# Two causal attentions: the multiplication of the exponentials by 1/sum moves from VectorE (DVE) to GpSimd (POOL)

## The chip, the cores and the metric

One Trainium2 chip, one of its cores. The metric is the device time of one execution in microseconds (us), taken as the median of several runs. The engines' names are those of the profile: PE is TensorE (matmuls and transposes), PEld its weight loads, DVE is VectorE, ACT is ScalarE, POOL is GpSimd, SP issues transfers.

## The reference

The program is a stack of four layers on 512 tokens of width 1024, all in float32. Layer 0 projects the tokens, selects keys with an indexer (top-k), attends with 8 heads of 64 and adds a short convolution; layer 1 is a latent attention with 16 heads; layers 2 and 3 are a differential and a neighbourhood attention. Layers 0 and 1 each end in an MLP. The change touches the softmax of layers 0 and 1 only. For each head and each block of 128 query rows the reference computes

```python
logits = jnp.where(causal[None, None], logits, -jnp.inf)
p = jax.nn.softmax(logits, axis=-1).astype(v.dtype)
return jnp.einsum('bhqs,bshd->bqhd', p, v)
```

Here the softmax is exp(scale * logit - max) divided by its sum over the keys; that division, done as a multiplication of the exponentials by a reciprocal, is what the change is about.

## The kernel before

The order of instructions on each engine is written out by hand: the program is emitted in one sequence, each engine executes its own instructions in the order in which they were emitted, and semaphores make an instruction wait for its inputs.

**Weights.** Every weight matrix comes from HBM in units of up to 128x1104 float32. `WeightStream.split` (L262) turns a unit into two halves: ACT rounds it (`w_hi`, L272) and POOL subtracts (`w_lo`, L273). A split is issued by `tick`, which `whole` calls after the matmuls of a piece of other work (L685). Splits run ahead of their use by a ring of four units.

**The attention.** `Net.causal` (L702) handles both attentions. A unit of its work is a head and a block of 128 query rows; block i sees (i+1)*128 keys, so a unit has 128, 256, 384 or 512 columns. Layer 0 has 8 heads x 4 blocks = 32 units (first all heads with blocks 0 and 1, then all with blocks 2 and 3), layer 1 has 16 x 4 = 64. The loop runs in steps; at step t five units are in work:

- A, the newest: PE computes the scores q.k into PSUM (`sp`);
- B, one step later: DVE adds the mask and takes the row maximum (L720, tile `at_nb`), ACT takes the exponential with its row sum (L406, `X<-sp,at_nb`);
- Dn, two steps later: DVE takes the reciprocal of the sum (L728, `at_rs`) and multiplies the exponentials by it in place (L730, `X<-X,at_rs`); the exponentials stand in one of three buffers `P`;
- T, three steps later: PE transposes the normalised block in pieces of 128 columns (L738, `tp`), ACT rounds the result (`pt`, L406), DVE subtracts for the low half (`low`, L409);
- G, four steps later: PE multiplies with v (L760, `mm`).

Within a step the code emits A, then T, then a piece of other matmuls (`fill`: convolution projections in layer 0, the next heads' q, k, v in layer 1) together with its weight split, then B and Dn interleaved: mask, reciprocal, exponential, multiplication. Then `s.due()` issues delayed work, among it what POOL does for the attention: the low halves `ql` of q (layer 1), `cvl` of the convolution (layer 0) and `yl` of the attention's output. Then come `low`, the evacuation of the piece, and G.

Of the kernel before, what the change touches and what calls it, by code (L numbers as in the profile page):

```python
# [16 lines left out]
OP = mybir.AluOpType  # L17
# [356 lines left out]
class Net:  # L374
# [327 lines left out]
    def causal(s, units, qk, scale, mask, vs, pt, out, P, tmp, ofs, wide, fill, extra=lambda t: None):  # L702

        nc = s.nc
        st, of, hold = {}, {}, {}
        N = len(units)

        def A(u):
            h, i = u
            n = max(256, (i + 1) * 128)  # L710
            ps = s.sp.tile([128, 512], F32, name="sp")
            qk(h, i, ps[:, :n], n)
            st[u] = {"s": ps, "n": (i + 1) * 128}

        def B(u, t):
            d = st[u]
            n = d["n"]
            d["P"] = P[t % 3]
            nb, d["sm"] = [s.rope.tile([128, 1], F32, name=f"at_{k}", bufs=4) for k in ("nb", "s")]
            nc.vector.tensor_tensor_reduce(d["s"][:, :n], d["s"][:, :n], mask(u[1]), -scale, 3e38, OP.add, OP.min, nb)  # L720
            yield
            s.act(d["P"][:, :n], d["s"][:, :n], AF.Exp, bias=nb, scale=-1.0, acc=d["sm"])
            yield

        def Dn(u):
            d = st[u]
            rs = s.rope.tile([128, 1], F32, name="at_rs", bufs=4)
            nc.vector.reciprocal(rs, d["sm"])  # L728
            yield
            nc.vector.tensor_scalar(d["P"][:, :d["n"]], d["P"][:, :d["n"]], rs, None, OP.mult)  # L730
            yield

        def T(u):
            h, i = u
            d = st[u]
            tp = s.tp.tile([128, 4, 128], F32, name="tp")
            for k in range(i + 1):
                nc.tensor.transpose(tp[:, k, :], d["P"][:, k * 128:(k + 1) * 128], s.ident)  # L738
            q = (i % 2) * 128
            H, L = [x[:, :i + 1, q:q + 128] for x in pt(h, i // 2)]  # L740
            s.act(H, tp[:, :i + 1, :], AF.Copy)
            d["lo"] = L, tp[:, :i + 1, :], H

        def low(u):
            if u:
                s.sub_lo(*st[u]["lo"])

        def G(u):
            h, i = u
            if i % 2 == 0:  # L750
                return
            c0, c1 = (0, 512) if wide else (i // 2 * 256, i // 2 * 256 + 256)
            if i == 1 or not wide:
                of[h] = s.mm.tile([128, 512], F32, name="mm")
            ps = of[h]
            o = ps[:, (i // 2) * 256:(i // 2) * 256 + 256]
            b = pt(h, i // 2)
            for k in range(i + 1):
                for w in range(2):
                    nc.tensor.matmul(o, vs(h, k), b[w][:, k, :], start=(k == 0 and w == 0), stop=(k == i and w == 1))  # L760
            if i == 3 or not wide:
                hp = (h % 2) * 64
                s.act(tmp[0:64, c0:c1], ps[64:128, c0:c1], AF.Copy)

                def add():
                    nc.vector.tensor_tensor(ofs[hp:hp + 64, c0:c1], ps[0:64, c0:c1], tmp[0:64, c0:c1], OP.add)

                def write():
                    H, L, f = out(h // 2, c0, c1, ofs[:, c0:c1])
                    s.act(H, f, AF.Copy)  # L770
                    s.sub_lo(L, f, H, nc.gpsimd)

                s.defer(add)
                if h % 2 == 1:
                    s.defer(write, 2)

        for t in range(N + 4):
            u = [units[t - k] if 0 <= t - k < N else None for k in range(5)]
            pcs = fill.get(t, [])
            if u[0]:  # L780
                A(u[0])
            if u[3]:
                T(u[3])
            for mm, _ in pcs:
                s.whole(mm)
            bb = B(u[1], t) if u[1] else iter(())
            dn = Dn(u[2]) if u[2] else iter(())
            for x in (bb, dn, bb, dn):
                next(x, None)
            s.due()  # L790
            low(u[3])
            for _, ev in pcs:
                ev()
            if u[4]:
                G(u[4])
                del st[u[4]]
            extra(t)
        s.drain()
# [1527 lines left out]
```

## Time and profile before

| | |
|---|---|
| time, median of 3 runs (range) | 3223.96 us (3220.66 to 3226.64) |
| the profiled execution | 3223.14 us, its span 3221.3 us |
| PE busy | 3067.4 us (95%) |
| DVE, ACT, POOL busy | 2132.6 (66%), 1605.0 (50%), 1473.9 us (46%) |
| attention of layer 0, 187 to 306 us | PE waits 5.6 us for the multiplication |
| attention of layer 1, 800 to 950 us | PE waits 14.4 us for the multiplication |

The two last rows are sums over the waits of PE in those stretches. The busy share of PE counts matmuls whose ends are modelled, so the waits say more about PE than the busy share does. The profiled execution took 1.8 us more than its span, which is the time before its first and after its last instruction, and it lies inside the range of the three runs.

### The profile page before, as it was taken

To read this page: it belongs to the slowest core of one execution; us is meant where nothing else is said; L and a number is where in the kernel's file an instruction comes from. 1 tells how busy PE (TensorE), PEld (TensorE's weight loads), DVE (VectorE), ACT (ScalarE), POOL (GpSimd) and SP (SyncE) were. 2 spreads that over 40 slices of the span, in tenths; PEclk is the share of its full clock that TensorE was granted. 3 is DMA by queue.
4 is the path that set the end of the run, shared out by engine and by line. 5 is a ranking of instruction groups with operands and counts; after the bars stand their busy time and mean duration, and the time that the engine had idled before them with its cause. 6 is when DMAs were issued, how large, how long until landed. Compare 5 with 4: busy or idle time off the path is not lost.

```text
span 3221.3 us, 58548 instructions
## 1 busy us (share of the span) xinstructions
PE 3067.4 (95%) x22868; PEld 2882.8 (89%) x22868; DVE 2132.6 (66%) x4241; ACT 1605.0 (50%) x3795; POOL 1473.9 (46%) x1296
## 2 busy tenths in 40 slices
PE   7999999998889999999999999998999999999989
PEld 7888889887788898789999999998999999999988
DVE  4886444556874344656777877788455777777864
ACT  4544533335665333455555555555325555555552
POOL 4432344443333444465544654462355444444444
PEclk9999999999999999999999999999999999999999
DMA  3122333433123344331221222123323322323334
GB/s 122 60 73 73 106 129 126 150 95 99 37 65 107 125 144 136 111 94 52 63 65 60 62 63 65 60 62 95 116 98 97 84 81 75 88 80 89 88 91 138
DMA packets 96128, 291.93 MB, mean 91 GB/s; under 512 B 19166, under 2 KB 28638, under 8 KB 92780
## 3 DMA queue, kind: packets, MB, share of 16 engines
q1 hardware_dynamic: 89148, 259.01, 24.8%
q0 software_dynamic: 5120, 25.17, 3.6%
q10 hardware_dynamic: 1584, 4.00, 0.4%
q8 instruction: 181, 2.97, 0.4%
q14 instruction: 95, 0.78, 0.1%
HBM read 244.05 MB, written 18.92 MB: 82 GB/s over the span
## 4 chain that ended last, share of the span: by engine, by line
PE 49%; DVE 13%; ACT 4%; issue 4%; DMA 3%; POOL 2%; SPq 0%; POOLq 0%; DVEq 0%; ACTq 0%
PE mm L578 13%; PE mm L580 12%; PE mm L579 12%; PE mm L2101 3%; DMA KL<-KL 1%; POOL w_lo L273 1%; PE tp L2239 1%; ACT X L406 1%; PE tp L2088 1%; DVE s L2051 1%; PE mm L2254 1%; PE mm L2249 1%; DVE X L2232 1%; PE s L2040 1%; DVE ge L1765 1%
## 5 line engine op out<-in xcount | busy, mean ns | idle before, releaser
L273 POOL TENSOR_TENSOR w_lo<-w_raw,w_hi 128x1024 fp32r<-128x1024 f32 (+2 forms) x350 | 879.0, 2517 | 1019.7 <-ACT w_hi L272 994.5
L578 PE MATMUL mm<-w_hi,hh 128*128 128x256 f32 (+3 forms) x2880 | 840.0, 292 | 7.9 <-ACT df_sq L406 2.6
L579 PE MATMUL mm<-w_lo,hh 128*128 128x256 f32 (+3 forms) x2880 | 820.3, 285 | 11.3 <-POOL w_lo L273 11.3
L580 PE MATMUL mm<-w_hi,hl 128*128 128x256 f32 (+3 forms) x2880 | 821.3, 285 | 3.3 <-POOL hl L409 3.0
L578 PEld LDWEIGHTS mm<-w_hi,hh 128*128 128x128 f32 x2880 | 550.5, 191 | 19.3 <-ACT df_sq L406 8.5
L579 PEld LDWEIGHTS mm<-w_lo,hh 128*128 128x128 f32 x2880 | 551.2, 191 | 18.4 <-POOL w_lo L273 13.8
L580 PEld LDWEIGHTS mm<-w_hi,hl 128*128 128x128 f32 x2880 | 549.6, 191 | 6.4 <-POOL hl L409 5.5
L272 ACT CAST w_hi<-w_raw 128x1024 fp32r<-128x1024 f32 (+2 forms) x355 | 366.1, 1035 | 206.0 <-PE mm L580 171.3
L578 PE MATMUL mm<-hh,w_hi 128*128 128x256 f32 (+1 forms) x1408 | 455.3, 323 | 3.0 <-DVE M L1083 2.8
L579 PE MATMUL mm<-hl,w_hi 128*128 128x256 f32 (+1 forms) x1408 | 448.3, 318 | 0.6
L580 PE MATMUL mm<-hh,w_lo 128*128 128x256 f32 (+1 forms) x1408 | 446.8, 317 | 1.2 <-DVE w_lo L273 1.2
L578 PEld LDWEIGHTS mm<-hh,w_hi 128*128 128x128 f32 x1408 | 265.9, 189 | 30.9 <-issue 5.2
L579 PE MATMUL mm<-w_lo,gh 128*128 128x256 f32 x1024 | 287.1, 280 | 1.4 <-POOL w_lo L273 1.4
L578 PE MATMUL mm<-w_hi,gh 128*128 128x256 f32 x1024 | 287.6, 281 | 0.0
L580 PE MATMUL mm<-w_hi,gl 128*128 128x256 f32 x1024 | 287.1, 280 | 0.1
L579 PEld LDWEIGHTS mm<-hl,w_hi 128*128 128x128 f32 x1408 | 265.9, 189 | 22.3 <-DVE hl L340 1.7
L580 PEld LDWEIGHTS mm<-hh,w_lo 128*128 128x128 f32 x1408 | 265.6, 189 | 21.9 <-DVE w_lo L273 1.6
L1262 DVE SCALAR_TENSOR_TENSOR macc<-modw,cg,macc 128x1024 f32<-128x1024 f32 x84 | 201.6, 2444 | 29.0 <-DMA modw<-in_mod 29.0
L579 PEld LDWEIGHTS mm<-w_lo,gh 128*128 128x128 f32 x1024 | 193.0, 188 | 1.9 <-POOL w_lo L273 1.6
L578 PEld LDWEIGHTS mm<-w_hi,gh 128*128 128x128 f32 x1024 | 193.3, 189 | 0.4
L580 PEld LDWEIGHTS mm<-w_hi,gl 128*128 128x128 f32 x1024 | 193.0, 189 | 0.5 <-DVE gl L409 0.5
L409 DVE TENSOR_TENSOR gl<-rsq,gh 128x512 fp32r<-128x512 f32 x64 | 45.6, 713 | 220.4 <-ACT gh L406 220.4
(373 smaller groups left out, 6880.4 us busy)
## 6 DMA issues: line engine op xcount, KB each, us to landing
w_raw<-in_w SPq DMA_DIRECT2D x336, 512.0 KB, 3.5
modw<-in_mod SPq DMA_DIRECT2D x24, 1024.0 KB, 5.8
KH<-KH POOLq DMA_DIRECT2D x32, 384.0 KB, 4.0
KL<-KL POOLq DMA_DIRECT2D x32, 384.0 KB, 5.1
xs<-X SPq DMA_DIRECT2D x12, 512.0 KB, 3.1
X<-xs SPq DMA_DIRECT2D x12, 512.0 KB, 6.7
yd<-ob SPq DMA_DIRECT2D x16, 384.0 KB, 2.3
w_raw<-in_w SPq DMA_DIRECT2D x8, 552.0 KB, 4.7
```

The source lines that it names most:

```text
L272: nc.scalar.copy(hi[:, :m], raw[:, :m])
L273: (eng or nc.gpsimd).tensor_tensor(lo[:, :m], raw[:, :m], hi.bitcast(F32)[:, :m], OP.subtract)
L406: return s.nc.scalar.activation(out, in_, func, bias=bias, scale=scale, **kw)
L409: (eng or s.nc.vector).tensor_tensor(lo, x, hi.bitcast(F32), OP.subtract)
L578: mm(ps, ah, bh, start=first, stop=False)
L579: mm(ps, ah, bl, start=False, stop=False)
L580: mm(ps, al, bh, start=False, stop=last)
L1262: nc.vector.scalar_tensor_tensor(acc[:, v], w[:, k2], cv, acc[:, v], OP.mult, OP.add)
L1765: nc.vector.reciprocal(x, x)
L2040: nc.tensor.matmul(o, q, KH[:, h, a:b], start=True, stop=False)
L2051: nc.vector.tensor_tensor_reduce(S, S, s.zero.to_broadcast(list(S.shape)), nrq[:, h:h + 1], 3e38, OP.add, OP.min, nb)
L2101: nc.tensor.matmul(ps, x["w"][:, k], V[g][:, kb, p * 128:(p + 1) * 128], start=k == 0, stop=k == nk - 1)
```

## The change

One line in `Dn`: the multiplication is issued on `nc.gpsimd` (POOL) and not on `nc.vector` (DVE). The reciprocal in front of it stays on DVE.

```diff
             nc.vector.reciprocal(rs, d["sm"])
             yield
-            nc.vector.tensor_scalar(d["P"][:, :d["n"]], d["P"][:, :d["n"]], rs, None, OP.mult)
+            nc.gpsimd.tensor_scalar(d["P"][:, :d["n"]], d["P"][:, :d["n"]], rs, None, OP.mult)
             yield
```

96 instructions leave DVE's order and 96 enter POOL's; the orders of PE and ACT are the same as before. On POOL, in layer 1, around the units of head 5 and the first two of head 6 (`X_66` and `X_67` are the tensors that hold the buffers `P`, the column count at the end tells the block; `w_lo` is a weight split, `ql` the low half of a q), the difference reads:

```order
 L409 TENSOR_TENSOR yl<-X_68,yh 128x8x64
-L273 TENSOR_TENSOR w_lo<-w_raw,w_hi 128x1024
+L730 TENSOR_SCALAR X_66<-X_66,at_rs 128x128
+L730 TENSOR_SCALAR X_66<-X_66,at_rs 128x256
+L273 TENSOR_TENSOR w_lo<-w_raw,w_hi 128x1024
+L730 TENSOR_SCALAR X_67<-X_67,at_rs 128x384
+L730 TENSOR_SCALAR X_66<-X_66,at_rs 128x512
 L409 TENSOR_TENSOR ql<-X_68,qh 128x512
+L730 TENSOR_SCALAR X_66<-X_66,at_rs 128x128
+L730 TENSOR_SCALAR X_67<-X_67,at_rs 128x256
 L409 TENSOR_TENSOR ql<-X_69,qh 128x512
```

The split stood between `yl` and `ql` with nothing else; now four multiplications stand around it, and that of block 2 (384 columns) comes right behind it.

On DVE, in layer 1, at a unit with 384 columns (`X_68<-mm,X_67` is the sum of the two halves of a head's output, `pt` the low half of a transposed block), the difference reads:

```order
 L409 TENSOR_TENSOR pt_8460<-tp,pt_8459 128x128
 L720 ISA sp,at_nb<-sp,m_7917 128x512
 L720 ISA at_nb 128x1
 L728 RECIPROCAL at_rs<-at_s 128x1
-L730 TENSOR_SCALAR X_66<-X_66,at_rs 128x384
 L766 TENSOR_TENSOR X_68<-mm,X_67 64x512
 L409 TENSOR_TENSOR pt_8460<-tp,pt_8459 128x2x128
```

The reciprocal is now followed at once by the work that stood behind the multiplication.

## Rows read from the trace of the kernel before

**Rows 1.** Page, busy time of each engine, its share of the span and instructions.
```profile
PE 3067.4 (95%) x22868; PEld 2882.8 (89%) x22868; DVE 2132.6 (66%) x4241; ACT 1605.0 (50%) x3795; POOL 1473.9 (46%) x1296
```
**Rows 2.** By stretch: start:end, length; PE, PEld, DVE, ACT, POOL busy; PEclk, DMA share, GB/s.
```profile
800.00:950.00 150.00, 129.80 (x803) 111.57 (x802) 133.93 (x377) 105.36 (x262) 51.16 (x31) 0.98 0.12 38
929.80:933.00 3.20, 3.20 (x17) 3.20 (x17) 3.11 (x11) 2.50 (x8) 0.00 (x0) 0.50 0.00 0
2560.00:3160.00 600.00, 567.04 (x4409) 547.84 (x4409) 462.02 (x953) 338.83 (x809) 274.38 (x271) 0.98 0.30 86
```
**Rows 3.** Waits of PE, 800 to 950 us: in total us, times, longest us.
```profile
PE tp L738 <- DVE X L730: 14.4, 20, 1.5
PE mm L760 <- DVE pt L409: 3.8, 7, 0.7
```
**Rows 4.** Waits of PE, 187 to 306 us.
```profile
PE tp L738 <- DVE X L730: 5.6, 6, 1.3
```
**Rows 5.** L730 on DVE, 187:306 and 800:953: count, busy us, mean ns, idle before.
```profile
L730 DVE TENSOR_SCALAR X<-X,at_rs 128x128 f32<-128x128 f32 (+3 forms) x32 | 18.3, 573 | 1.4
...
L730 DVE TENSOR_SCALAR X<-X,at_rs 128x128 f32<-128x128 f32 (+1 forms) x64 | 42.5, 664 | 2.7
```
**Rows 6.** Instructions of L730, 800 to 953 us: duration ns min/median/max, first and last start.
```profile
L730 DVE TENSOR_SCALAR X<-X,at_rs x64: 285/452/1646, 802.7 to 947.1; 128x128 f32<-128x128 f32 x16, 128x256 f32<-128x256 f32 x16, 128x384 f32<-128x384 f32 x16, 128x512 f32<-128x512 f32 x16
```
**Rows 7.** Timeline at 843 us: start, us, engine, instruction [idle before <-releaser].
```profile
843.24 1.55 DVE L730 TENSOR_SCALAR X<-X,at_rs 128x384 f32<-128x384 f32 x1
843.27 1.31 POOL L409 TENSOR_TENSOR ql<-X,qh 128x512 fp32r<-128x512 f32 x1 [4.29 <-DVE at_rs L728]
```
**Rows 8.** Chain that ended last, 840 to 860 us, shares by line.
```profile
by line: DVE X L730 18.2%; DVE sp L720 11.5%; DVE X L1401 10.4%; DVE pt L409 9.0%; PE mm L580 8.3%; PE mm L578 8.1%; PE mm L579 8.0%; DVE kl L409 6.8%; PE mm L760 5.5%; PE tp L738 4.2%; issue 4.2%; DVE X L766 3.4%; DVE at_nb L720 1.5%; DVE 
```
**Rows 9.** Timeline, 852 to 857 us, units of head 5.
```profile
852.43 1.04 ACT L272 CAST w_hi<-w_raw 128x1024 fp32r<-128x1024 f32 x1
...
853.55 2.41 POOL L273 TENSOR_TENSOR w_lo<-w_raw,w_hi 128x1024 fp32r<-128x1024 f32 x1 [4.01 <-ACT w_hi L272]
...
854.19 0.49 PE L738 MATMUL tp<-ident,X 128*128 128x128 f32 x3
...
856.39 0.63 PE L738 MATMUL tp<-ident,X 128*128 128x128 f32 x4 [0.70 <-DVE X L730]
```
**Rows 10.** Instructions of L273, 800 to 953 us.
```profile
L273 POOL TENSOR_TENSOR w_lo<-w_raw,w_hi x10: 1286/2388/2422, 814.6 to 936.5; 128x1024 fp32r<-128x1024 f32 x8, 128x512 fp32r<-128x512 f32 x2
```
**Rows 11.** Timeline of POOL, the first and the last of those ten.
```profile
814.61 2.39 POOL L273 TENSOR_TENSOR w_lo<-w_raw,w_hi 128x1024 fp32r<-128x1024 f32 x1 [7.91 <-ACT w_hi L272]
...
936.54 2.38 POOL L273 TENSOR_TENSOR w_lo<-w_raw,w_hi 128x1024 fp32r<-128x1024 f32 x1 [8.37 <-ACT w_hi L272]
```
**Rows 12.** Timeline of PE, the transposes that follow these two.
```profile
815.29 0.49 PE L738 MATMUL tp<-ident,X 128*128 128x128 f32 x3
...
937.65 0.38 PE L738 MATMUL tp<-ident,X 128*128 128x128 f32 x2
```
**Rows 13.** Instructions of L273, 190 to 306 us.
```profile
L273 POOL TENSOR_TENSOR w_lo<-w_raw,w_hi x10: 2373/2397/2468, 198.7 to 283.1; 128x1024 fp32r<-128x1024 f32 x10
```
**Rows 14.** Timeline of layer 0: a split on POOL, the transposes behind it on PE.
```profile
283.12 2.39 POOL L273 TENSOR_TENSOR w_lo<-w_raw,w_hi 128x1024 fp32r<-128x1024 f32 x1 [1.70 <-ACT w_hi L272]
...
285.11 0.55 PE L738 MATMUL tp<-ident,X 128*128 128x128 f32 x3
```
**Rows 15.** Groups on POOL by shape, whole span: count, busy us, mean ns, idle before.
```profile
L409 POOL TENSOR_TENSOR ql<-X,qh 128x512 fp32r<-128x512 f32 x16 | 20.8, 1302 | 33.8 <-DVE at_rs L728 25.9 <-ACT qh L406 4.6 <-DVE X L730 3.3
L1793 POOL CAST QS<-QS 128x128 fp32r<-128x128 f32 x16 | 4.6, 293 | 26.4 <-DVE QS L1791 26.4
L1680 POOL CAST VS<-X 128x384 fp32r<-128x384 f32 x7 | 3.6, 516 | 0.0
```
**Rows 16.** Instructions of L849, the only scaling on POOL.
```profile
L849 POOL TENSOR_SCALAR wi<-tk x4: 255/372/488, 67.9 to 77.5; 128x16 f32<-128x16 f32 x4
```
**Rows 17.** Waits of PE, 2560 to 3160 us.
```profile
PE tp L2239 <- DVE X L2232: 26.8, 20, 3.5
```

## The prediction, made before the changed kernel ran

> **What bounds the kernel now.** I read the busy times first: PE is busy 95% of the span [rows 1], so what lengthens this program is time in which PE has to wait, and what shortens it is such a wait gone. Next the table by stretch: in layer 1's attention PE is busy 129.8 of 150 us, DVE 133.9, ACT 105.4, POOL 51.2 [rows 2]. POOL has room by this sum; whether it has room at the right moments the sum does not tell. Then the waits of PE there. The transposes of a normalised block wait for the multiplication L730 20 times, 14.4 us in all, and PE waits another 3.8 us for the low half `pt`, which stands behind the multiplication on DVE [rows 3]; in layer 0 the first kind is 5.6 us in 6 waits [rows 4]. So the multiplication is already what PE waits for in both attentions, and there is at most 14.4 + 3.8 + 5.6 = 23.8 us to gain.
>
> Part of that wait is not work. L730 takes 42.5 us on DVE in layer 1 and 18.3 us in layer 0 [rows 5], with a shortest instruction of 0.285 us, a median of 0.452 and a longest of 1.646 [rows 6]. The timeline shows one of the long ones: started at 843.24, a POOL subtraction started at 843.27 and ended at 844.58, and the multiplication ended 0.21 us after it, having taken 1.55 us [rows 7]. DVE was held while POOL worked. The Trainium skill, "SBUF — State Buffer", section "Who interferes with whom", says that GpSimd's SBUF ports are VectorE's second pair and that whoever takes them holds them for the whole instruction; this trace agrees.
>
> Last, the order of POOL and its timeline. The change puts a multiplication right behind most weight splits. That decides the sum.
>
> **The change part by part.** Removed from DVE: 96 instructions, 42.5 + 18.3 = 60.8 us. Added to POOL: the same 96. The reciprocal stays, the transposes wait for POOL now, and nothing moves on PE, ACT or SP's queue.
>
> *What one multiplication costs on POOL.* The trace shows no scaling of this size there. From below: a cast, also one tensor read and one written, takes 0.293 us for 128 columns and 0.516 for 384 [rows 15], 0.87 ns per column; the only scaling on POOL takes at least 0.255 us for 16 columns [rows 16], 0.06 above that line. That gives 0.35, 0.47, 0.58 and 0.69 us for 128 to 512 columns. From above: a subtraction of two tensors takes 1.302 us for 512 [rows 15], and a line from 0.255 us up to it gives 0.49, 0.76, 1.03 and 1.30. I take the middle, 0.42, 0.61, 0.80 and 0.99 us, as both rows are equally near, and keep both ends. The Trainium skill, "GPSIMD Engine Reference", section "4.1 Engine selection", says that GpSimd is about 2x slower on two inputs and roughly at line rate on one. The cast rows agree; by that rule the lower line holds and the sum below ends at 3254 us.
>
> *What stands in front of it.* In a step with a split the code emits transposes of the unit before, ACT's rounding of them, ACT's cast of the weights, POOL's split, and then this unit's multiplication. Head 5, block 2: cast at 852.43 for 1.04 us, split from 853.55 to 855.96 [rows 9]. The multiplication can end at 855.96 + 0.80 = 856.76, and with the 0.15 us that pass today from its end to the transpose, PE can start at 856.91. PE is there at 854.19 [rows 9]: a wait of 2.72 us where there is none. It cannot be hidden by the delay of earlier units, because the cast follows the transposes of the unit before and shifts with them. Layer 1 has ten such splits, eight of 1024 columns and two of 512 [rows 10]. The first ends at 817.00 and PE comes at 815.29: 817.00 + 0.80 + 0.15 - 815.29 = 2.66; the last (256 columns) 938.92 + 0.61 + 0.15 - 937.65 = 2.03 [rows 11, 12]. The same working over all ten gives 2.66, 2.12, 2.72, 2.72, 1.97, 1.29, 2.69, 3.61, 2.66 and 2.03, together 24.5 us. In return seven units next to a split, which wait today because DVE is held by it, have their result before PE arrives; the one of head 5 is the 0.70 us before 856.39 [rows 9], all seven are 4.5 us. Net +20.0.
>
> *The other units of layer 1.* Of their 14.4 - 4.5 = 9.9 us of today's waits little goes. Where `yl` or `ql` stands in front on POOL, the multiplication starts when that ends, as DVE's does today in effect [rows 7], and is 0.1 to 0.5 us longer. Unit by unit (end of reciprocal or of POOL's instruction in front, plus the cost, plus 0.15, against PE's arrival, less the shift that the unit before has brought) I get 18.1: +8.2. Behind `ql` and `yl` on POOL nothing is queued that PE needs within two steps.
>
> *Layer 0.* Ten splits stand in front of multiplications [rows 13]. One ends at 285.51, PE comes at 285.11 [rows 14]: 285.51 + 0.80 + 0.15 - 285.11 = 1.35 us. Its steps are longer, so more is covered: the 32 units wait 12.6 us by the same working, against 5.8 now (5.6 and a few waits too short to be listed). Net +6.9.
>
> Together +35.1; with the lower prices +29.1, with the upper +41.4.
>
> *What DVE gives back.* The low halves `pt` come earlier by the multiplication, so that 3.8 us [rows 3] should go nearly whole; earlier reciprocals take perhaps 4 us more from units that wait for nothing else. I take -8, bounds -11 and 0.
>
> *The hand-over.* A POOL instruction that waits starts some 0.08 us after its releaser (cast end 853.47, split 853.55 [rows 9]) where I counted 0.04: about 40 waits x 0.05 = +2.
>
> *The clock.* TensorE's granted clock in 800 to 950 us is 0.98, and in 929.8 to 933.0 it is 0.50 (1.2 of 2.4 GHz) while PE works without a break [rows 2]. What more waits cost I take from layer 3, where PE waits 20 times, the longest 3.5 us [rows 17], and the clock is 0.98 over 600 us [rows 2]: about 12 us lost, 0.6 per wait. Some 14 new waits of over 1.2 us: +8. Bounds: 0 if none is followed by the lower level; 14 x 1.6 = 22 if all are.
>
> Sum: 35.1 - 8 + 2 + 8 = +37 us. The profiled execution took 3223.1 us (span 3221.3 and 1.8 around it), 0.8 below the median of the runs, well within their spread. Forecast: 3260 us. Its own range, from the ends: 29 - 11 = +18, so 3241, and 41 + 2 + 22 = +65, so 3288.
>
> **The rivals.**
>
> *Faster: DVE's relief decides.* In 840 to 860 us L730 is the largest item of the chain that ended last, 18.2%, and the chain runs mostly over DVE [rows 8]; DVE is busier than PE there. If POOL finished each multiplication before PE came, all 23.8 us of waits would go: 3199 us. It decides from the point at which the splits no longer stand between the cast and the multiplication, or PE comes later than them by itself. Against: the order of POOL, and 855.96 against 854.19.
>
> *No change.* Relief and queueing cancel, within 6 us of 3223. That needs the relief at 23.8 us and the ten waits at half of what I work out, for instance because ACT, freed from waiting for DVE, casts the weights a microsecond sooner. For: ACT's exponentials do wait for DVE. Against: the cast at 852.43 has no idle time before it [rows 9]; ACT is at work and not waiting.
>
> *Much slower: the scaling on POOL costs twice the upper line.* Its mean would be 1.8 us, 64 x 1.8 + 51 = 166 us of POOL work in 150 us: POOL would bound layer 1. Each of the 96 units would be about 0.9 us later than at the upper line, some two thirds of them in the open: +60 on top of +44, 3327 us. For: one scaling of 16 columns took 0.488 us [rows 16]. Against: the cast rows.
>
> That the change does not do what it says is excluded by the order: 96 instructions leave DVE and the same 96 stand on POOL.
>
> **How the numbers follow.** The forecast has 0.82, faster 0.06, no change 0.06, much slower 0.06. A difference under 0.2%, 6.4 us, cannot be told from none here. The slow cases are all slower: 0.88. Same 0.06, faster 0.06. The range for 8 in 10 leaves out the three rivals but for their edges and the outer ends of the forecast, where several bounds would have to meet: 3238 to 3282 us.
>
> **What would show it.** Right: L730 on POOL with 0.35 to 1.0 us; PE's transposes waiting for `X` L730 of POOL, about 43 us in layer 1 and 13 in layer 0; ten of these at 1.3 to 3.6 us right behind a `w_lo`; waits for `pt` nearly gone; DVE less busy by 61 us, and the rest of the span, outside both attentions, unchanged. Wrong: the transposes waiting for L730 no longer than today, or POOL's multiplications starting at the end of the reciprocal in the steps with a split; L730 far above 1.3 us at 512 columns would make the third rival the case.

## The result, and the profile after

The changed kernel takes 3274.27 us (median of four runs, 3268.77 to 3276.03), the kernel before 3224.14 us beside it. The ratio is 1.0154, with a 95% interval of 1.0138 to 1.0170: slower, inside the predicted range and 14 us above the predicted 3260 us. The profiled execution took 3268.8 us with a span of 3266.9 us, 45.6 us longer than the 3221.3 us of the kernel before. It is the fastest of the four; the text returns to the other three at the clock.

The page's busy times, answering to [rows 1]:

```profile
PE 3081.1 (94%) x22868; PEld 2891.6 (89%) x22868; DVE 2072.4 (63%) x4145; ACT 1602.5 (49%) x3795; POOL 1574.1 (48%) x1392
```

DVE is relieved of 60.2 us and of 96 instructions, POOL has 100.2 us and 96 instructions more. The work moved as the change says, and it is dearer where it went. By shape, what L730 costs on POOL (groups of instructions: count, busy us, mean ns, idle time before):

```profile
L730 POOL TENSOR_SCALAR X<-X,at_rs 128x512 f32<-128x512 f32 x24 | 37.6, 1565 | 12.7 <-DVE at_rs L728 12.1 <-PE tp L738 0.6
L730 POOL TENSOR_SCALAR X<-X,at_rs 128x384 f32<-128x384 f32 x24 | 30.1, 1252 | 1.9 <-DVE at_rs L728 1.9
L730 POOL TENSOR_SCALAR X<-X,at_rs 128x256 f32<-128x256 f32 x24 | 22.4, 932 | 37.9 <-DVE at_rs L728 29.4 <-PE mm L580 8.5
L730 POOL TENSOR_SCALAR X<-X,at_rs 128x128 f32<-128x128 f32 x24 | 14.5, 604 | 6.3 <-DVE at_rs L728 6.3
```

604 to 1565 ns: each is above the upper bound that the prediction had drawn, 0.49 to 1.30 us. What it does to PE is in PE's waits, first over layer 1's attention (812 to 998 us), then over layer 0's (187 to 316 us):

```profile
PE tp L738 <- POOL X L730: 40.5, 29, 3.7
...
PE mm L760 <- DVE pt L409: 1.0, 3, 0.3
...
PE tp L738 <- POOL X L730: 15.4, 14, 1.8
```

Against 14.4 us in 20 waits [rows 3] and 5.6 in 6 [rows 4]. Over both attentions, the waits too short to be listed among them, it is 56.0 us after and 20.2 before: +35.8. In exchange the wait for `pt` in layer 1 shrank from 3.8 us [rows 3] to 1.0.

One of the ten places behind a split, the same unit as in [rows 9] (head 5, block 2), on the timeline:

```profile
876.62 0.16 DVE L728 RECIPROCAL at_rs<-at_s 128x1 f32<-128x1 f32 x1
877.41 1.04 ACT L272 CAST w_hi<-w_raw 128x1024 fp32r<-128x1024 f32 x1
878.53 2.40 POOL L273 TENSOR_TENSOR w_lo<-w_raw,w_hi 128x1024 fp32r<-128x1024 f32 x1 [2.56 <-ACT w_hi L272]
879.12 0.28 PE L580 MATMUL sp<-kh,ql 128*128 128x256 f32 x1
880.92 2.77 POOL L730 TENSOR_SCALAR X<-X,at_rs 128x384 f32<-128x384 f32 x2
882.21 0.55 PE L738 MATMUL tp<-ident,X 128*128 128x128 f32 x3 [2.81 <-POOL X L730]
```

The reciprocal was there at 876.78. From then on POOL could have multiplied, and it did nothing: it stood idle in front of the subtraction, which waits for ACT's cast (2.56 us in all, 1.75 of them after the reciprocal), then subtracted for 2.40 us, and only then came to the multiplication (two of them in one row: this unit's 1.24 us and the next one's). PE waited 2.81 us; in the kernel before it did not wait at this place.

The clock, by stretch (columns as in [rows 2]), for 150 us of layer 1 and for two short pieces in it:

```profile
812.00:962.00 150.00, 114.86 (x615) 97.46 (x615) 76.20 (x247) 82.50 (x204) 95.35 (x76) 0.89 0.11 34
833.20:836.60 3.40, 3.40 (x15) 3.11 (x14) 1.02 (x5) 2.04 (x6) 2.86 (x3) 0.50 0.25 102
908.30:911.70 3.40, 3.40 (x14) 3.10 (x13) 1.30 (x5) 2.25 (x7) 2.69 (x3) 0.50 0.27 108
```

PE is busy 114.9 of 150 us instead of 129.8, and the granted clock is 0.89 instead of 0.98 [rows 2]. The two pieces at 0.50 (1.2 of 2.4 GHz) follow transposes that began at 832.71 and 907.65 us, after waits of 2.63 and 2.64 us. Of the ten long waits behind a split in layer 1 seven are followed so, within 1.6 us of their end; in an eighth the clock had fallen during the wait, and after two it did not fall.

**The account of the span.** All idle time of PE went from 148.8 to 180.8 us (+32.0). The time at half clock (granted clock 0.50) went from 69.4 us in 18 pieces to 95.6 us in 23 (+26.2); at half speed half of it is lost, +13.1. Together +45.1, against 45.6 us of longer span. This sum (change of PE's idle time plus half the change of the time at half clock) gives the change of the span within 1.6 us in twelve of the thirteen changed kernels below, so nothing large in PE's time lies outside these two terms; in the thirteenth, the second mixture, it is 3.2 us off.

Where the time went can be read by setting the same matmuls of PE side by side (those that it starts from 187 to 306 and from 800 to 985 us in the kernel before). Layer 0's attention is 10.8 us longer and layer 1's 37.6; they hold 3.4 and 30.7 us more at half clock. The stretches outside, whose instructions are unchanged, hold 7.9 us less of it. So much can differ between two executions whatever the edit: over all executions on record the mean granted clock of the kernel before is 0.987 to 0.993, that of the changed kernel 0.983 to 0.985. Some us in the half-clock column below are therefore no effect of an edit by themselves.

### The profile page after: what moved, and what is told of

It reads as the page before. It is cut to its first block, busy times and chain, and to the rows that moved or that the text cites. A ratio compares the mean times of both kernels' runs of the same rounds, so it can differ in the third digit from the quotient of the medians.

```text
span 3266.9 us, 58578 instructions
## 1 busy us (share of the span) xinstructions
PE 3081.1 (94%) x22868; PEld 2891.6 (89%) x22868; DVE 2072.4 (63%) x4145; ACT 1602.5 (49%) x3795; POOL 1574.1 (48%) x1392
## 4 chain that ended last, share of the span: by engine, by line
PE 48%; DVE 11%; issue 5%; ACT 4%; POOL 4%; DMA 3%; SPq 0%; POOLq 0%; ACTq 0%; DVEq 0%
PE mm L578 12%; PE mm L580 12%; PE mm L579 12%; PE mm L2101 3%; POOL w_lo L273 2%; ACT X L406 1%; DMA KL<-KL 1%; PE tp L2239 1%; PE tp L2088 1%; POOL X L730 1%; DVE s L2051 1%; PE mm L2249 1%; PE mm L2254 1%; PE s L2040 1%; PE s L2041 1%
## 5 line engine op out<-in xcount | busy, mean ns | idle before, releaser
L273 POOL TENSOR_TENSOR w_lo<-w_raw,w_hi 128x1024 fp32r<-128x1024 f32 (+2 forms) x350 | 878.3, 2515 | 983.6 <-ACT w_hi L272 955.1
L579 PE MATMUL mm<-w_lo,hh 128*128 128x256 f32 (+3 forms) x2880 | 818.0, 284 | 12.1 <-POOL w_lo L273 11.7
L409 DVE TENSOR_TENSOR gl<-rsq,gh 128x512 fp32r<-128x512 f32 x64 | 45.6, 712 | 220.4 <-ACT gh L406 220.4
```

Source lines behind the costliest of these rows:

```text
L273: (eng or nc.gpsimd).tensor_tensor(lo[:, :m], raw[:, :m], hi.bitcast(F32)[:, :m], OP.subtract)
L409: (eng or s.nc.vector).tensor_tensor(lo, x, hi.bitcast(F32), OP.subtract)
L579: mm(ps, ah, bl, start=False, stop=False)
```

## The experiments

Every kernel computes the whole output. PE's waits for the multiplication are sorted by where the unit stands: in layer 1 the ten units whose step issues a split, the ten in the step behind it and the other 44, then layer 0's 32. All columns but the ratio are in us; those from "split step" on are of the profiled execution. The ratio's 95% interval is to the kernel before, run on the same chip.

| kernel | us | ratio, interval | split step | step behind | other | layer 0 | waits in all | PE idle | half clock |
|---|---|---|---|---|---|---|---|---|---|
| before | 3224.14 | | 0.0 | 4.5 | 10.0 | 5.8 | 20.2 | 148.8 | 69.4 |
| changed | 3274.27 | 1.0138 to 1.0170 | 26.3 | 0.4 | 13.8 | 15.4 | 56.0 | 180.8 | 95.6 |
| subtraction late (POOL) | 3239.43 | 1.0037 to 1.0067 | 0.0 | 13.4 | 15.7 | 10.0 | 39.1 | 162.7 | 75.3 |
| layer 0 only | 3235.98 | 1.0023 to 1.0053 | 0.0 | 4.3 | 9.8 | 13.5 | 27.6 | 153.7 | 86.4 |
| broadcast product | 3251.06 | 1.0070 to 1.0103 | 22.4 | 0.0 | 12.4 | 10.3 | 45.1 | 171.9 | 75.4 |
| mixture 1 | 3242.33 | 1.0045 to 1.0075 | 0.0 | 13.0 | 16.1 | 8.4 | 37.5 | 166.9 | 78.6 |
| subtraction on DVE | 3271.16 | 1.0125 to 1.0157 | 23.0 | 3.1 | 14.8 | 11.7 | 52.6 | 175.6 | 116.9 |
| the same, broadcast | 3251.23 | 1.0067 to 1.0096 | 20.3 | 1.7 | 11.7 | 10.9 | 44.7 | 170.5 | 95.9 |
| late and broadcast | 3226.23 | 0.9990 to 1.0011 | 0.0 | 9.2 | 13.4 | 6.5 | 29.2 | 154.8 | 66.1 |
| mixture 2 | 3228.72 | 0.9998 to 1.0016 | 0.0 | 4.6 | 16.5 | 7.1 | 28.2 | 150.2 | 82.3 |
| late on DVE | 3251.00 | 1.0068 to 1.0104 | 0.0 | 17.7 | 16.7 | 12.0 | 46.4 | 172.6 | 75.3 |
| late on DVE, broadcast | 3232.47 | 1.0018 to 1.0036 | 0.0 | 12.5 | 14.6 | 9.0 | 36.1 | 161.1 | 66.2 |
| whole split late, broadcast | 3243.58 | 1.0043 to 1.0079 | 0.0 | 16.8 | 11.8 | 9.4 | 38.0 | 165.4 | 82.4 |
| mixture 3 | 3219.07 | 0.9978 to 0.9995 | 0.0 | 5.1 | 13.3 | 5.5 | 23.9 | 148.7 | 61.8 |

Two theories stood at the start. **Q, the queue:** the price is the place of the multiplication behind a split on POOL. **D, the duration:** the price is POOL's longer multiplication, wherever it stands.

**Subtraction late (POOL).** POOL subtracts behind the step's multiplication instead of ahead of it: `split` puts its subtraction into the list `late`, which is run behind it.

```diff
+            late = []
             for mm, _ in pcs:
-                s.whole(mm)
+                for _ in mm() or ():
+                    pass
+                s.W.tick(late=late)
...
             for x in (bb, dn, bb, dn):
                 next(x, None)
+            for f in late:
+                f()
```

> Q (queue order: most of the loss is multiplications that stand behind a weight split on POOL). The multiplication stays on POOL, but in a step with a split POOL's subtraction is issued behind it; ACT's cast stays where it is. The ten waits of 2.1 to 3.7 us in layer 1 and the nine in layer 0 go; part comes back one unit later, whose multiplication now stands behind the subtraction (about 1.2 us for the wide splits of layer 1). Waits of PE 56 -> about 35 us, with the clock some 27 us less than the changed kernel: 3247 us. D (duration: POOL takes 0.60 to 1.57 us where DVE takes 0.29 to 0.49, and the order does not matter): no change, 3270 to 3277 us.

3239.43 us. Not one instruction is shorter, and 34.8 of the 50.1 us are gone: Q, and against D. It even overshot Q's 3247. The 26.3 us in the split steps went to zero, but 13.4 us appeared one step later, which neither theory had. The timeline of POOL, DVE and PE there:

```profile
844.98 2.42 POOL L274 TENSOR_TENSOR w_lo<-w_raw,w_hi 128x1024 fp32r<-128x1024 f32 x1 [0.34 <-ACT w_hi L272]
...
845.73 0.49 PE L741 MATMUL tp<-ident,X 128*128 128x128 f32 x3
...
846.39 0.16 DVE L731 RECIPROCAL at_rs<-at_s 128x1 f32<-128x1 f32 x1
...
847.37 1.56 POOL L733 TENSOR_SCALAR X<-X,at_rs 128x512 f32<-128x512 f32 x1
...
848.99 0.66 PE L741 MATMUL tp<-ident,X 128*128 128x128 f32 x4 [1.77 <-POOL X L733]
```

POOL no longer idles in front of the subtraction for long (0.34 us), since the cast has had time. But the next unit's reciprocal ends at 846.55 in the middle of it, its multiplication starts 0.82 us later and takes 1.56 us, and PE waits 1.77 us.

**Layer 0 only.** Layer 1's multiplication goes back to DVE.

```diff
-            nc.gpsimd.tensor_scalar(d["P"][:, :d["n"]], d["P"][:, :d["n"]], rs, None, OP.mult)
+            eng = nc.gpsimd if wide is False else nc.vector
+            eng.tensor_scalar(d["P"][:, :d["n"]], d["P"][:, :d["n"]], rs, None, OP.mult)
```

> The multiplication is on POOL in layer 0's attention only, layer 1 is as before. Q: by the waits of the changed kernel layer 0 gives +9.7 us of waits, less 0.5 us of waits for the low half, plus 2 to 3 us by the clock: 3235 us. D: in proportion to the units, a third of +50: 3241 us. If the two layers do not add up (layer 0 shifts something that layer 1 pays for), under 3229 us.

3235.98 us: Q's number to a microsecond. Layer 0's part is some 12 us and layer 1's some 38, and the parts act where they stand: layer 1's waits are those of before (14.1 against 14.4 us). Of layer 0's 14.6 us of longer span 4.9 are idle time of PE and 8.5 clock (17.0 us more at half clock).

**Broadcast product.** The same multiplication, written as a product of two tensors, the reciprocal read as a broadcast.

```diff
-            nc.gpsimd.tensor_scalar(d["P"][:, :d["n"]], d["P"][:, :d["n"]], rs, None, OP.mult)
+            nc.gpsimd.tensor_tensor(d["P"][:, :d["n"]], d["P"][:, :d["n"]], rs.to_broadcast([128, d["n"]]), OP.mult)
```

> The multiplication on POOL is written as a product of two tensors with the reciprocal broadcast along the row; same place in the order. The row of POOL's broadcast product of 768 columns (1.47 us) suggests about 1.0 to 1.1 us for 512 columns where the scaling takes 1.57. Q: only the part of each wait that is the multiplication itself shrinks, 43 waits by some 0.25 us: 3262 us. D: POOL's work falls from 104.6 to about 75 us, the loss with it from 50 to 28: 3252 us.

```profile
L730 POOL TENSOR_TENSOR X<-X,at_rs 128x512 f32<-128x512 f32 x24 | 25.0, 1041 | 15.0 <-DVE at_rs L728 14.9
...
L730 POOL TENSOR_TENSOR X<-X,at_rs 128x128 f32<-128x128 f32 x24 | 9.7, 403 | 6.8 <-DVE at_rs L728 6.8
```

A third shorter at every width, 34.9 us of POOL's time less. The time, 3251.06 us, is D's number, but not by D's way: PE's idle time fell by 8.9 us, as Q had it, and the rest is the clock (20.2 us less at half clock, 10.1 us). The four executions bear that out: their mean granted clock is 0.986 to 0.988, where the changed kernel has 0.983 to 0.985. The ten waits behind a split are still 22.4 us (26.3 before this edit): a cheaper multiplication only shortens the tail of each. So the length has a price of its own beside the place; Q alone does not give this time.

**Mixture 1.** In the 20 steps that issue a split DVE multiplies, in the other 76 POOL: `Dn` takes `nc.vector` where its new argument is true, else `nc.gpsimd`.

```diff
+            was = s.W.halved
...
-            dn = Dn(u[2]) if u[2] else iter(())
+            dn = Dn(u[2], s.W.halved > was) if u[2] else iter(())
```

> In a step that issues a weight split the multiplication is done by DVE, in all others by POOL. Q: no multiplication stands behind a split any more; waits of PE about 20 us as before the change, 3218 to 3230 us. D: about three quarters of the multiplications are still on POOL, so three quarters of the loss: 3262 us.

3242.33 us, between the two and expected by neither. The split steps are free, but the step behind holds 13.0 us, as in the first experiment: a split's subtraction takes 2.40 us and reaches into the next unit. Q in its first form, "the multiplication of its step", was too narrow.

**Subtraction on DVE,** in place, in the two attentions; and **the same, broadcast.** The edit is `s.W.tick(nc.vector)` for the tick inside `s.whole(mm)`, in the second with the product of above.

> The changed kernel (multiplication on POOL, tensor_scalar), but in the two attentions the subtraction of each weight split is done by DVE instead of POOL; nothing is left out. Theory Q (the dear waits are the multiplications queued behind a split's subtraction on POOL): the units that waited behind a split (26.3 us in layer 1, some 4 us more in layer 0) fall to the 0.6 us of an undisturbed unit, and so do the units one step later, so that TensorE's waits for the multiplication fall from 56.0 to 18 to 25 us; DVE takes on twenty subtractions of some 1.1 us, which costs a few us of its own. Time 3222 to 3232 us. Theory D (the dearer multiplication itself, 604 to 1565 ns against DVE's 285 to 452 ns and more, is what costs, wherever it stands in the queue): waits stay above 40 us and the time above 3255 us.

> As the run before it, with POOL's multiplication as a tensor_tensor against the broadcast reciprocal (403 to 1041 ns instead of 604 to 1565 ns); nothing is left out. Theory Q: with the splits out of POOL's queue the only thing left is the length of the multiplication, of which most units hide all: waits of 12 to 18 us, 3216 to 3226 us, so at or a little under the kernel before. Theory D: the gain against the run before is a third of the multiplication's time, as it was between the changed kernel and its broadcast version, some 20 us, wherever the splits are: 3235 us if the run before it stands at 3255 us.

3271.16 us: Q missed by some 40 us. Time and waits are in D's range, but D does not explain them either, as the timeline of a split step shows:

```profile
855.46 1.04 ACT L272 CAST w_hi<-w_raw 128x1024 fp32r<-128x1024 f32 x1
...
856.53 1.23 DVE L273 TENSOR_TENSOR w_lo<-w_raw,w_hi 128x1024 fp32r<-128x1024 f32 x1 [2.79 <-ACT w_hi L272]
857.67 0.69 DVE L720 CUSTOM_DVE_ANT_0 sp<-sp,m 128x512 f32<-128x512 f32 x1
...
858.28 0.16 DVE L728 RECIPROCAL at_rs<-at_s 128x1 f32<-128x1 f32 x1
...
858.64 1.25 POOL L730 TENSOR_SCALAR X<-X,at_rs 128x384 f32<-128x384 f32 x1 [3.99 <-DVE at_rs L728]
...
859.94 0.55 PE L738 MATMUL tp<-ident,X 128*128 128x128 f32 x3 [2.38 <-POOL X L730]
```

The queue has only changed engines. Now DVE stands 2.79 us in front of the subtraction, waiting for the cast, and the mask and the reciprocal stand behind it; POOL is idle for 3.99 us and starts as soon as the reciprocal comes. The unit waits 2.38 us, on POOL's side it was 2.68 at the same place (head 3, block 2). With the broadcast product it was 3251.23 us, 19.9 less: what D expected for the difference, but again 10.5 of the 16.1 us of shorter span are clock, and the ten waits are still 20.3 us.

**Late and broadcast.** The first and the third experiment together.

> Two edits together, nothing left out: POOL issues each split's subtraction behind the step's multiplication, and the multiplication is the broadcast tensor_tensor. Each edit alone gave -34.8 us (order) and -23.2 us (broadcast) against the changed kernel. If both act on the same waits (theory Q: waits behind a split), they add up only in part: 3226 to 3234 us, since the eight units of the next step still wait behind the late subtraction (13.4 us in all with the order alone, some 9 us here). If they act on different things (theory D: the queue and the length each have their price), they add up: 3212 to 3220 us.

3226.23 us, level with the kernel before, inside Q's interval and not in D's: both edits act in part on the same waits. 9.2 us are left in the step behind a split, expected were some 9.

**Mixture 2.** DVE multiplies in the split steps and in the step behind each (38 units), POOL in the other 58: `Dn(u[2], now or prev)`.

> The multiplication goes to DVE in the steps that issue a split and in the step behind each of them, and to POOL in all other steps; nothing is left out. Theory Q2 (a split's subtraction delays two multiplications, that of its step and that of the next): against the version that sent only the split's own step to DVE (3242.3 us, 37.4 us of waits, 12.9 us of them in eight units one step behind a split), those 12.9 us shrink to 3 to 5 us: waits of 27 to 30 us and a time of 3228 to 3235 us. Theory Q1 (the eight waits had another cause, the share of DVE's own queue): no change, 3240 to 3245 us.

3228.72 us, and the step behind fell from 13.0 to 4.6 us, about what it is in the kernel before. So a split delays two multiplications. Who waits for which engine (us, times; first for DVE's, then for POOL's):

```profile
  PE tp L741: 9.4, 14
...
  PE tp L741: 18.6, 21
```

**Late on DVE,** and **late on DVE, broadcast.** The subtraction on DVE, behind the step's evictions: `s.W.tick(nc.vector, late)`, the list run after `ev()`.

> The changed kernel (multiplication on POOL, tensor_scalar), but in the two attentions the subtraction of each weight split goes to DVE and stands behind the step's bias, reciprocal and evictions instead of ahead of them; nothing is left out. With the subtraction on DVE but ahead of them the time was 3271.2 us and the ten waits stayed at 2.35 to 3.46 us. Theory O (order: whatever stands behind the subtraction on an in-order engine waits for ACT's cast too, on DVE as on POOL): those ten waits go to zero as they did with POOL's subtraction issued late (3239.4 us), and the next step's 1.1 to 2.5 us shrink, because DVE's subtraction takes 1.23 us against POOL's 2.40 us: waits for the multiplication of 27 to 32 us, time 3227 to 3236 us. Theory L (load: a DVE that takes on the subtractions is late with the bias and the reciprocal wherever they stand): waits above 40 us, time above 3250 us.

> As the run before it, with the broadcast tensor_tensor as POOL's multiplication; nothing is left out. Theory O: POOL's queue is free of splits and what is left is the multiplication's length and POOL's evictions (ql, yl, cvl) in front of it: waits of 18 to 24 us, about the 20.2 us + 5.0 us that the kernel before spends on multiplication and pt, so 3216 to 3226 us, level with it or a little faster. Theory L: 3235 us or more.

3251.00 and 3232.47 us: O missed both times. The first is L's number in time and in waits (46.4 us, O had 27 to 32); the second lies between O's 3226 and L's 3235, with 36.1 us of waits where O had 18 to 24. Each theory holds for a part of the waits. The ten in the split step, which had been 0.97 to 3.46 us with the subtraction on DVE ahead of the step's work, are zero, as O said, with the same multiplication and the same load on DVE: in the pair above the place of the subtraction made them. But the step behind rose to 17.7 us where I had expected less than 13.4. There the load on DVE counts, as the timeline of that step shows:

```profile
851.16 0.49 PE L741 MATMUL tp<-ident,X 128*128 128x128 f32 x3
...
851.62 1.22 DVE L274 TENSOR_TENSOR w_lo<-w_raw,w_hi 128x1024 fp32r<-128x1024 f32 x1
...
852.96 0.16 DVE L731 RECIPROCAL at_rs<-at_s 128x1 f32<-128x1 f32 x1
...
853.29 1.56 POOL L733 TENSOR_SCALAR X<-X,at_rs 128x512 f32<-128x512 f32 x1 [3.31 <-DVE at_rs L731]
...
854.91 0.66 PE L741 MATMUL tp<-ident,X 128*128 128x128 f32 x4 [2.25 <-POOL X L733]
```

DVE's subtraction is half as long as POOL's, but on DVE it delays the reciprocal, and the whole multiplication still follows. From the start of the transposes of the unit before to the end of this reciprocal pass 1.96 us (851.16 to 853.12); in the first experiment, at the same unit, it was 0.82 (845.73 to 846.55). On POOL the subtraction had run beside the reciprocal, and only its rest was in the way.

**Whole split late, broadcast.** The cast, too, is issued at the end of the step: `s.W.tick()` behind `ev()`.

> POOL multiplies with the broadcast tensor_tensor and subtracts, and in the two attentions the whole weight split (ACT's cast and POOL's subtraction) is issued at the end of the step, behind the evictions; nothing is left out. Against the version with POOL's subtraction alone issued late (3226.2 us, 29.2 us of waits) only the place of ACT's cast differs, and the subtraction stands a little later. If the cast ahead of the exponentials costs something of its own (1.04 us on ACT, up to twenty times), waits fall below 24 us and the time to 3212 to 3222 us. If the wait in POOL's queue is all there is to it, nothing is gained, and the later subtraction delays the next step more: 3226 to 3240 us.

3243.58 us, 17.4 more than with the subtraction alone late and 3.6 above even the upper end of what was expected. Nothing is gained by moving the cast; moved back, it makes POOL subtract later still, and the step behind goes from 9.2 to 16.8 us. Whether the cast ahead of the exponentials costs something smaller is not shown, since a gain would be covered by this loss.

**Mixture 3.** Subtraction late on POOL, broadcast product on POOL, DVE's multiplication in the step behind a split.

> Three edits on the changed kernel, nothing left out: in the two attentions POOL issues a split's subtraction behind the step's multiplication; POOL's multiplication is the broadcast tensor_tensor; and in the step behind a split DVE multiplies instead. Against the version with the first two edits (3226.2 us, 29.2 us of waits for the multiplication), the eleven units one step behind a split (13.6 us of waits there, 6.1 us in the kernel before, where DVE multiplies) fall to about 6 us. If the price of a split is paid only through POOL's queue: waits of 20 to 23 us, 3214 to 3223 us, level with the kernel before or 0.1 to 0.3 per cent under it. If DVE, held by POOL's late subtraction at the shared port, loses as much again (in the kernel before a multiplication beside POOL's work took 1.55 us instead of 0.42 us): waits of 27 us or more and 3225 to 3232 us.

3219.07 us, a ratio of 0.9986 (0.9978 to 0.9995) to the kernel before: the only version under it, by some 4 us. PE's waits in layer 0 (first two rows) and in layer 1:

```profile
PE tp L744 <- DVE X L734: 3.3, 4, 1.3
PE tp L744 <- POOL X L736: 2.1, 3, 1.2
...
PE tp L744 <- POOL X L736: 13.3, 13, 1.9
PE tp L744 <- DVE X L734: 5.1, 8, 1.2
```

The waits, 23.9 us with the short ones, are not fewer than the kernel before has; PE's idle time is the same, 148.7 us. The profiled execution has 7.6 us less at half clock, but only 3.4 of these lie in layer 1's attention and none in layer 0's; the rest lies where the instructions are unchanged. Over all executions the mean granted clock is 0.987 to 0.991 here and 0.988 to 0.991 for the kernel before beside it. So where the 4 us come from is not shown, and they are less than the 0.2% that the prediction set as its limit. DVE did not lose its multiplications to POOL's late subtraction: 5.1 us in the step behind, 4.5 before.

## Why the prediction held, step by step

| step of the sum | predicted | measured in the profile |
|---|---|---|
| ten units behind a split, layer 1 | +24.5 | +26.3 |
| seven units next to a split, no longer held | -4.5 | -4.1 (the ten in the step behind: 4.5 to 0.4) |
| other units of layer 1 | +8.2 | +3.8 |
| layer 0 | +6.9 | +9.6 |
| DVE's relief | -8 | -4.0 (PE's waits for `pt`, 6.1 to 2.1 in the program) |
| hand-over | +2 | within the waits above |
| clock | +8 | +13.1 |
| other idle time of PE, rounding | | +0.4 |
| sum | +37 | +45.1; span +45.6 |

- *The mechanism held.* The multiplications stand behind the splits, PE finds them late, and the ten waits are 2.63, 2.24, 2.68, 2.81, 2.13, 2.64, 2.76, 3.71, 2.63 and 2.07 us against the ten that were worked out; nine of ten are within 0.2 us. The exception is the sixth, 2.64 for 1.29: PE came there 2.13 us after the start of the cast, where it had come 3.16 us after it in the kernel before. That the place in the queue is the cause of these ten waits, and not the length of the multiplication, is shown by the first experiment, which moves nothing but the place and brings them to zero. Of the whole loss the place is the larger part, 34.8 of 50.1 us; the length has a price of its own, 23.2 us by the third experiment, and the two overlap.
- *The price of one multiplication was mis-sized.* It is 0.60 to 1.57 us where 0.42 to 0.99 was taken and 0.49 to 1.30 was the upper bound; of the signs of being right, "0.35 to 1.0 us" did not come. The bound was drawn from another form of instruction, a subtraction of two tensors; the broadcast product, which is of that form, lies under it. The waits hardly show the error, because two other numbers were off the other way; that they came out so close is luck in this part. At head 5, block 2 the multiplication was 0.44 us dearer than taken. From its end to the transpose passed 0.06 us (882.15 to 882.21) where 0.15 was counted; and PE arrived 1.99 us after the start of the cast, not 1.76 as in [rows 9]. 2.72 + 0.44 - 0.09 - 0.23 = 2.84, measured 2.81.
- *The other units and the hand-over.* The other units of layer 1 rose less than half of what was worked out (3.8 for 8.2), and why stays open. The hand-over does not give it: it is 0.09 us shorter from POOL to PE, but from the reciprocal's end to a waiting multiplication's start pass 0.17 us (median of 29) where 0.08 was taken.
- *The Trainium skill's rule did not hold for this form.* "GPSIMD Engine Reference", section "4.1 Engine selection", has one-input work roughly at line rate on GpSimd; here the form with one tensor and one scalar per partition was the slowest of the three at 512 columns, 1.57 us against 1.30 for the subtraction of two tensors and 1.04 for the broadcast product. The 3254 us that the rule gave was too low.
- *The relief was over-sized.* The `pt` waits went as expected (3.8 us, measured 4.0), but the 4 us from earlier reciprocals did not show. A likely reason, which no run tests, is that the units that waited for nothing else now wait for POOL.
- *The clock was under-sized.* 0.6 us for each long wait had been read from layer 3 [rows 17]; here the loss was nearly 1 for each of the 14 (waits over 1.2 us: 19 after, 5 before), and in the two attentions alone 17 us, 1.2 each. In the three runs that were not profiled the mean granted clock was 0.983 instead of 0.985 with spans of 3270.9 to 3274.3 us; that alone makes some (0.985 - 0.983) x 3270 = 6.5 us, about the 5.5 us by which the median lies above the profiled run.
- *The rivals.* DVE's relief did not decide: it came to 4 us. The much slower case had its condition half met, L730 above 1.3 us at 512 columns, but its mean is 1.09 us and not 1.8, and POOL did not bound layer 1: 95.4 of 150 us busy.

## What to carry to other kernels

Before moving an instruction to an engine with room, read what stands in front of it in that engine's order and what that in turn waits for: here 2.4 us of work and the idle waiting for a third engine in front of it made waits of 2.1 to 3.7 us for multiplications of 0.6 to 1.6 us, and every other place of the same subtraction that was tried, on either engine, put something of the chain behind it. An idle share is no room if the queue stands still in it. Change the order or the form of the instruction first (34.8 and 23.2 us here, 48 together) and move single units rather than all, each to the engine that is free at that step. Even so the best version here is only 0.14% under the kernel that leaves every multiplication on DVE: relieving DVE bought next to nothing in this kernel.

## What the runs showed of the hardware

- On POOL a `tensor_scalar` with a scalar per partition in float32 took 604, 932, 1252 and 1565 ns for 128 to 512 columns (2.50 ns per further column), the same product as `tensor_tensor` with a broadcast operand 403, 621, 836 and 1041 ns (1.66 ns per column).
- A transpose waiting for POOL started 0.05 to 0.06 us after POOL's end in all 43 waits, where the kernel before shows 0.15 us after DVE's in 25 of 26. (The ends of POOL's instructions in the profile are rough.)
- The same subtraction of 128x1024 took 1.22 us on DVE and 2.40 us on POOL.
- The granted clock of one execution is a loose measure. The profiled execution of the version with the subtraction on DVE has 3.4 us less waits than that of the changed kernel and 21.3 us more at half clock, in 33 pieces instead of 23; but 10.2 of these lie behind layer 1's attention, where the instructions are the same, and over four executions each the mean clock is 0.982 to 0.985 and 0.983 to 0.985, no difference. Of all terms of a forecast this one stays the least certain.
